# Weight splits ordered behind the steps of a recurrence, weights fetched earlier, and the samples' state products moved by a step: one layer of an RWKV-7 / short-convolution decoder

## The chip, the cores and the metric

The kernel runs on one core of a Trainium2 chip. The engines are TensorE (PE: matrix products; PEld its weight loads), VectorE (DVE: elementwise work), ScalarE (ACT: elementwise functions and copies), GpSimd (POOL) and SyncE (SP), whose queue issues most copies from DRAM. The metric is the device time of one execution in microseconds. PSUM is the memory that PE writes; it is shared out here in banks of 128 x 512 fp32.

## The reference: what is computed

One layer of a decoder, on 512 prompt tokens and on 8 samples of 4 tokens each (544 columns in all), fp32, model width 1024:

```python
x = layer_norm(ALPHA * x + 0.5 * swiglu(x, ffn1...))
proj = x @ w_in                          # 3328 columns: r, k, v, decay, a, gate | conv B, C, h
# RWKV-7: per head (8 heads of 64), per token
sa = S @ (-kk);  S = S * w + sa (kk*a)^T + v k^T;  o = S @ r
# group norm of o, bonus term, gate -> y_rwkv ; short convolution of width 3 -> y_conv
x = layer_norm(ALPHA * x + concat(y_rwkv, y_conv) @ w_out)
x = layer_norm(ALPHA * x + 0.5 * swiglu(x, ffn2...))
```

The outputs are the layer's result and the new states (the matrices S, the last shifted row, the last rows of the convolution), for the prompt and for the samples.

## The kernel before

Activations lie transposed: 128 rows of the model width on the partitions, tokens along the free axis, in two halves of 256 and 288 columns (`HALF`). Every large product is made of three matmuls: each fp32 operand is split in a high and a low part (both in PE's faster fp32r type), and high x high, high x low and low x high are summed. So each tile of weights (128 x 1024 fp32, 512 KB) is loaded into a raw buffer (`raw`, two of them in this part of the kernel), and then split by `wsplit`: ACT writes the high part (L135), DVE the low part, raw minus high (L136), into a tile `hl` (three of them, a fourth from the end of the first recurrence on). `wload` asks for the copy and the split; `wget` does so once for each tile of `w_in`. The low part's subtraction is what sets the raw buffer free for the next copy. `mm3` issues the matmuls of one output half: for 8 row blocks 24 matmuls, the low weights in every third of them (L154).

Between the two feed-forward blocks lies the mixer. The RWKV state recurrence is done by chunks of 64 tokens: for each of two groups of four heads (g = 0, 1) eight steps, `chain`, each of them a chain PE -> ACT -> PE -> DVE and ACT -> PE -> DVE:

- L1230: products of S (and of v) with the chunk's scores; ACT copies the result to W (L1233)
- L1239: W times the chunk's triangular inverse; DVE copies one half of the result into UV (L1240), ACT the other half (L1241)
- L1248: the state product; DVE adds it to S (L1256) and scales it (L1258). This last one is `upd` in the code
- L1209 and L1215: the chunk's outputs, of the step before; ACT copies them (L1217)

While the chain waits, PE gets other work, the fill: generators in a queue `bg`, from which `take(n)` draws about n ns of matmuls. `slots` alternates: it lets the chain write one step, then takes fill for that step (1500 in the recurrences). In recurrence 0 the fill is the projection for the convolution (`conv`, three tiles of `w_in` for each of four blocks: C, h, B, through `conv_mm`, each tile for both halves); in recurrence 1 it is the first part of the output product (`wout0`: for d = 0 to 7 four blocks of convolution rows from `wo_c[d // 2]`, and two blocks from `wo_0[d // 4]`), then `wout1` for the second half of the tokens. `last0` follows after recurrence 1 with the remaining two blocks. The pairs' own projections (`own_a`, `own_b`) are put in front of that queue where a pair of heads is due.

The samples (`sample`) are worked in between: `recur` calls `small(c, k)` at three places of each step c, which by a table `when` draws one or two pieces of the samples' work: two groups of 32 state products (L1293, one group for each pair of heads), copies, two small products, and then for each pair the new state (`ux` L1330, a product L1333, DVE L1335 and L1336). Two thirds into the recurrence the group norm of the first 256 tokens (`gnorm`, L1349 to L1369) is drawn too; that of the other 288 follows behind the recurrence.

The order of instructions on an engine is set by a scheduler when the program is built: among the instructions that it holds for ready by its own clock it takes the one that was written first. Two means hold it to an order on one engine: `after(a, b)` (a behind b) and `tc.issue_after(b)` (all that the block writes behind b). `slots` uses the second: the chain's matmuls are put behind the last fill matmul, and what a `take` writes is put behind the last product of the step on PE, and on ACT and DVE behind `seen["old"]`, the UV copy and the state product of the step before the one just written. The engines run the order as it was built, each instruction waiting for its operands.

Of the kernel before, what the change touches and what calls it, by code (L numbers as in the profile page):

```python
# [15 lines left out]
OP = mybir.AluOpType  # L16
# [45 lines left out]
def body(ctx: ExitStack, tc: tile.TileContext, xT, gu1, wd1, win, wo_c, wo_0, wo_1, gu2, wd2, wl, ln3, eye, lora, vec, cst,  # L62
# [71 lines left out]
    def wsplit(hl, raw, a, b):  # L134
        seen["hi"] = ACT.activation(hl[:, 0, a:b], raw[:, a:b], AF.Copy)  # L135
        seen["lo"] = DVE.tensor_tensor(hl[:, 1, a:b], raw[:, a:b], hl[:, 0, a:b].bitcast(F32), op=OP.subtract)  # L136
        return seen["lo"]

    def split(hi, lo, x):
# [16 lines left out]
                yield 6 * ((c1 - c0) / 2.4 + 3)  # L156

    bg = deque()
    seen = dict(rs=None, hhl=None, pe=None, fill=None, uv=None, new=[], old=[])

    def crit(e):
        seen["pe"] = e
# [1032 lines left out]
    def chain(g, cp, small):  # L1195


        tl = cp.tile
        AR = ARs[g]
        heads = [(pl, par) for pl in range(2) for par in range(2)]  # L1200
        Ss, q2, uv = {}, None, []

        def at(q, pl, par):
            return q[R(par), pl * 64:pl * 64 + 64]

        def out_u(c):
            q = sm()
            for pl, par in heads:
                crit(PE.matmul(at(q, pl, par), UV[:, pl, par, c, :], SC[:, pl, par, c, 64:128], start=(pl == 0 or c == 0),  # L1209
                               stop=(c == 0), skip_group_check=True))  # L1210
            return q

        def out_s(c, q):
            for pl, par in heads if c else ():
                crit(PE.matmul(at(q, pl, par), Ss[c][R(par), pl, par, :], AR[R(par), pl, c, 1, :], start=False, stop=True,  # L1215
                               skip_group_check=True))
            o = ACT.activation(O[:, :, c, :], v2(q), AF.Copy)  # L1217
            for e in uv:
                after(o, e)

        for c in range(8):
            if c < 7:
                Sn = Ss[c + 1] = tl([P, 2, 2, 64], F32, name="S", bufs=3)
                with tc.issue_after(seen["pool"].ins):
                    for par in range(2):
                        POOL.tensor_copy(Sn[R(1 - par), :, par, :], UV[R(1 - par), :, par, c + 1, :])
            q = sm()
            for pl, par in heads:
                k = slice(0, P) if c else R(1 - par)
                crit(PE.matmul(at(q, pl, par), SC[k, pl, par, c, 0:64], Ss[c][:, pl, par, :] if c else UV[k, pl, par, c, :],  # L1230
                               start=True, stop=True))
            W = tl([P, 2, 64], F32, name="W", bufs=2)
            ACT.activation(W, v2(q), AF.Copy)  # L1233
            if c:
                q2 = out_u(c - 1)
            small(c, 0)
            qs = (sm(), sm())
            for pl, par in heads:
                crit(PE.matmul(at(qs[par], pl, par), XT[R(par), c, pl, :], W[R(par), pl, :], start=True, stop=True))  # L1239
            seen["uv"] = DVE.tensor_copy(UV[R(0), :, 0, c, :], v2(qs[0], R(0)))  # L1240
            seen["new"] = [ACT.copy(UV[R(1), :, 1, c, :], v2(qs[1], R(1)))]  # L1241
            uv[:] = seen["new"]
            if c:
                out_s(c - 1, q2)
            small(c, 1)
            q = sm()
            for par, pl in heads:
                crit(PE.matmul(at(q, pl, par), BK[:, pl, par, c, :], UV[:, pl, par, c, :], start=True, stop=True))  # L1248
            pe = Pe[:, 2 * g:2 * g + 2, c:c + 1].to_broadcast([P, 2, 64])
            if c == 7:  # L1250
                SF = tl([P, 2, 64], F32, name="W", bufs=2)
            for par in range(2):
                dst = Sn[R(par), :, par, :] if c < 7 else SF[R(par)]
                src = v2(q, R(par))
                if c:
                    DVE.tensor_tensor(dst, Ss[c][R(par), :, par, :], src, op=OP.add)  # L1256
                    src = dst
                upd = DVE.tensor_tensor(dst, src, pe[R(par)], op=OP.mult)  # L1258
            seen["new"].append(upd)
            small(c, 2)  # L1260
            if c == 7:
                dma(wkvp_o[:, 2 * g:2 * g + 2, :], SF)
                out_s(7, out_u(7))
            yield 1

    def recur(g, cp, run):
        sam, gn = sample(g, cp), gnorm(g, 0, cp)
        when = {(2, 0): 1, (2, 1): 1, (2, 2): 1, (3, 0): 1, (3, 1): 1, (4, 2): 1, (5, 2): 2, (6, 2): 2}

        def small(c, k):  # L1270
            for _ in range(when.get((c, k), 0)):
# [9 lines left out]
    def sample(g, cp):  # L1281
# [3 lines left out]
        dma(S0, s0[:, 2 * g:2 * g + 2])  # L1285
        WT = tl([P, 2, 32], F32, name="WT")
        SI = tl([P, 2, 2, 64], F32, name="SI")
        q = sm()
        qv = q[:, :256].rearrange("p (d x t) -> p d x t", d=2, x=2)
        for pl in range(2):  # L1290
            for b in range(NSEQ):
# [48 lines left out]
    def gnorm(g, h, cp):  # L1340
# [13 lines left out]
            PE.matmul(q[:, :n], bo, sq[pl][:, :n], start=True, stop=True)  # L1354
            ACT.activation(sq[pl][:, :n], q[:, :n], AF.Ln, scale=1.0 / 64, bias=epsg)
        for pl in range(2):
            ACT.activation(sq[pl][:, :n], sq[pl][:, :n], AF.Exp, scale=-0.5)
        yield 600
        for pl in range(2):
            p = 2 * g + pl  # L1360
# [2 lines left out]
        for pl in range(2):  # L1363
            p, y = 2 * g + pl, sq[pl]
            DVE.scalar_tensor_tensor(y[:, :n], xc[pl][:, :n], col(V_GNG, p), sq[pl][:, :n], op0=OP.mult, op1=OP.mult)
            DVE.scalar_tensor_tensor(y[:, :n], y[:, :n], col(V_GNB, p), bvs[g][pl][:, t0:t1], op0=OP.add, op1=OP.add)
            DVE.tensor_tensor(o[pl], y[:, :n], qs[pl][:, :n], op=OP.mult)
            if g == 0:
                dma(ycd[:, p, t0:t1], o[pl])  # L1369
            else:  # L1370
# [19 lines left out]
    def conv(i):  # L1390
# [3 lines left out]
        us = u[:, 514:].rearrange("p (b t) -> p b t", t=6)  # L1394
        POOL.memset(u[:, 0:2], 0.0)
        POOL.tensor_copy(us[:, :, 0:2], cst_[:, i])
        for h in range(2):
            yield from conv_mm(14 + 3 * i, h, partial(conv_c, cc))
        for h in range(2):
            yield from conv_mm(15 + 3 * i, h, partial(conv_u, cc, u, us))  # L1400
        taps = conv_taps(i, u, us, zc)
        next(taps)
        for h in range(2):
            for n, x in enumerate(conv_mm(16 + 3 * i, h, partial(conv_z, zc))):
                if n in (0, 2):
                    next(taps, None)
                yield x
            for _ in taps:
                pass
        dma(ycd[:, 4 + i], zc)  # L1410

    def conv_mm(i, h, use):
        c0, c1 = HALF[h]
        w = wget(i)
        q = big()
        yield from mm3(q[:, :c1 - c0], w, xhl, range(KD), c0, c1)
        use(q, h, c0, c1)
        yield 300
# [80 lines left out]
    w4 = pool(ast, "w4")  # L1499
    wstate["ex_hl"] = [lambda: w4.tile([P, 2, 1024], F32R, name="hl", bufs=1)]  # L1500
    weave("s2", pairs[2].scores())
    bg.appendleft(own_b(3))
    need(3, 2)
    take(FILL["p3"])
# [42 lines left out]
            for k, y in ys + [(7, zc)]:  # L1547
                ysplit(k, y, c0, c1)

    w1s, fin = {}, []  # L1550

    def add_z(d, h, o, n=1):
        c0, c1 = HALF[h]
# [3 lines left out]
    def wout0():  # L1557
# [10 lines left out]
        for d in range(2):  # L1568
            yield from mm3(os[d][:, :c1], wc, xhl, (4, 5, 6, 7), c0, c1, d * 4, stop=False)
        for d in range(KD):  # L1570
            if d == 4:
                w0 = wload(wo_0[1])
            if d > 1:
                if d % 2 == 0:
                    wc = wload(wo_c[d // 2])
                o = big()
                yield from mm3(o[:, :c1], wc, xhl, (4, 5, 6, 7), c0, c1, (d % 2) * 4, stop=False)
            else:
# [20 lines left out]
    def wout1():  # L1599
# [8 lines left out]
        for d in range(KD):  # L1608
            if d == 4:
                w0 = wload(wo_0[1])  # L1610
            if d % 2 == 0:
                wc = wload(wo_c[d // 2])
            if d == 0:
                w0 = wload(wo_0[0])
            all_in = 3 in fin
            while all_in and rest:
                o = big()
# [48 lines left out]
    ast.close()  # L1666
    mst.close()
    yst.close()

    f2.s1[0] = s1  # L1670
    f2.open()
# [97 lines left out]
```

## Time and profile before

| | us |
|---|---|
| median of 3 runs | 1072.5 (1072.36 to 1072.72) |
| profiled execution: its time | 1072.43 |
| profiled execution: its span, first to last instruction | 1070.7 |
| recurrence 0: first L1230 to the last step's state product | 503.9 to 543.6 |
| recurrence 1 | 617.5 to 657.8 |
| a high part (ACT L135, mean of 230) | 1.02 |
| a low part (DVE L136, mean of 230) | 1.18 |
| granted clock of PE | 0.998 |

Rows of the timeline show start, duration, engine, line, operation, out <- in with shapes, a count where neighbours of one kind are merged, and in brackets how long the engine had idled and what released it. The durations of neighbours on one engine overlap by some tenths of a microsecond, because an instruction enters the pipe as the one before it leaves; what one costs in a row of work is the distance of the starts. PE's ends are modelled. A row of the waits names who waited, for whom, us in total, times, the longest.

### The profile page before, as it was taken

What the parts mean: (1) busy time and instruction counts of PE and PEld (TensorE: products, weight loads), DVE (VectorE), ACT (ScalarE), POOL (GpSimd) and SP (SyncE); (2) the same over time, 40 slices, a digit from 0 to 9 for tenths busy, and PEclk for the clock granted to TensorE, in tenths of its full rate; (3) what the DMA queues carried; (4) which work ended last, traced back from release to release, by engine and by line L of the source; (5) the groups of instructions that cost most, each with busy time, mean ns of one, the idle gap of its engine ahead of it and who ended that gap; (6) DMA issues with size and microseconds to landing.
All of it is one profiled execution on the core that took longest, in us unless ns stands there. A gap on an engine that the chain in (4) does not pass through costs nothing.

```text
span 1070.7 us, 22612 instructions
## 1 busy us (share of the span) xinstructions
PE 1050.7 (98%) x9178; PEld 1010.5 (94%) x9178; DVE 844.7 (79%) x1557; ACT 583.2 (54%) x1070; POOL 154.9 (14%) x273
## 2 busy tenths in 40 slices
PE   9999999999999999999999999999999999999997
PEld 8999999999999999899889988999999999999996
DVE  6797888979875777793578657988979888797757
ACT  5746555555553668654444435767555555555524
POOL 0111121211200022133101200001211212121000
PEclk9999999999999999999999999999999999999999
DMA  8558585676854233324145724434766848668512
GB/s 292 132 112 186 120 199 135 145 172 132 186 118 158 79 88 109 85 82 99 41 143 161 173 81 139 141 119 79 152 165 137 200 101 194 143 137 189 147 43 84
DMA packets 91528, 144.48 MB, mean 135 GB/s; under 512 B 34848, under 2 KB 52384, under 8 KB 91296
## 3 DMA queue, kind: packets, MB, share of 16 engines
q1 hardware_dynamic: 68144, 110.76, 34.2%
q0 software_dynamic: 22848, 31.72, 19.2%
q8 instruction: 72, 1.18, 0.4%
q10 hardware_dynamic: 432, 0.56, 0.2%
q14 instruction: 32, 0.26, 0.1%
HBM read 128.81 MB, written 9.75 MB: 129 GB/s over the span
## 4 chain that ended last, share of the span: by engine, by line
PE 76%; DVE 13%; ACT 7%; issue 2%; DMA 2%; POOL 0%; ACTq 0%; DVEq 0%; SPq 0%
PE mm L553 9%; PE mm L554 9%; PE mm L555 9%; PE sm L553 6%; PE sm L554 6%; PE sm L555 6%; PE mm L152 6%; PE mm L153 5%; PE mm L154 5%; DVE hhl L141 2%; ACT hl L135 2%; DVE hl L136 2%; PE sm L441 1%; PE sm L1166 1%; PE mm L784 1%
## 5 line engine op out<-in xcount | busy, mean ns | idle before, releaser
L136 DVE TENSOR_TENSOR hl<-raw,hl 128x1024 fp32r<-128x1024 f32 (+3 forms) x230 | 270.2, 1179 | 63.7 <-ACT hl L135 62.6
L135 ACT ACTIVATE hl<-raw 128x1024 fp32r<-128x1024 f32 (+3 forms) x230 | 232.9, 1020 | 69.7 <-DVE raw L519 43.5
L152 PE MATMUL mm<-xhl,hl 128*128 128x256 f32 (+1 forms) x704 | 209.2, 299 | 0.5 <-ACT xhl L140 0.5
L153 PE MATMUL mm<-xhl,hl 128*128 128x256 f32 (+1 forms) x704 | 203.0, 289 | 0.4 <-DVE xhl L141 0.4
L154 PE MATMUL mm<-xhl,hl 128*128 128x256 f32 (+1 forms) x704 | 202.0, 287 | 0.0
L152 PEld LDWEIGHTS mm<-xhl,hl 128*128 128x128 f32 x704 | 132.0, 188 | 6.9 <-issue 2.0
L153 PEld LDWEIGHTS mm<-xhl,hl 128*128 128x128 f32 x704 | 132.3, 188 | 2.7 <-issue 1.0
L154 PEld LDWEIGHTS mm<-xhl,hl 128*128 128x128 f32 x704 | 132.3, 188 | 0.3 <-issue 0.2
L555 PE MATMUL sm<-xhl,hl 128*128 128x272 f32 x432 | 125.2, 290 | 0.0
L554 PE MATMUL sm<-xhl,hl 128*128 128x272 f32 x432 | 124.4, 288 | 0.0
L553 PE MATMUL sm<-xhl,hl 128*128 128x272 f32 x432 | 124.1, 287 | 0.0
L553 PE MATMUL mm<-tv,hl 128*128 128x272 f32 x288 | 83.3, 289 | 0.3
L555 PE MATMUL mm<-tv,hl 128*128 128x272 f32 x288 | 83.4, 290 | 0.0
L554 PE MATMUL mm<-tv,hl 128*128 128x272 f32 x288 | 83.1, 288 | 0.0
L553 PEld LDWEIGHTS sm<-xhl,hl 128*128 128x128 f32 x432 | 81.4, 188 | 0.0
L554 PEld LDWEIGHTS sm<-xhl,hl 128*128 128x128 f32 x432 | 81.3, 188 | 0.0
L555 PEld LDWEIGHTS sm<-xhl,hl 128*128 128x128 f32 x432 | 81.2, 188 | 0.0
L532 POOL DMA_DIRECT2D raw<-in_wd x32 | 39.2, 1462 | 288.0 <-DVE hlb L141 225.2
L526 POOL DMA_DIRECT2D raw<-in_gu x36 | 43.3, 1203 | 203.5 <-DVE hlb L141 143.8
L553 PE MATMUL mm<-hhl,hl 128*128 128x272 f32 x192 | 56.4, 300 | 0.3
L554 PE MATMUL mm<-hhl,hl 128*128 128x272 f32 x192 | 55.9, 291 | 0.8 <-DVE hhl L141 0.2
L553 PEld LDWEIGHTS mm<-tv,hl 128*128 128x128 f32 x288 | 54.2, 188 | 1.9 <-ACT cpb L620 1.9
(416 smaller groups left out, 2716.0 us busy)
## 6 DMA issues: line engine op xcount, KB each, us to landing
raw<-in_gu SPq DMA_DIRECT2D x84, 512.0 KB, 4.5
raw<-in_gu POOLq DMA_DIRECT2D x36, 512.0 KB, 6.6
raw<-in_wd SPq DMA_DIRECT2D x32, 512.0 KB, 4.5
raw<-in_win SPq DMA_DIRECT2D x26, 512.0 KB, 3.6
raw<-in_wd POOLq DMA_DIRECT2D x32, 256.0 KB, 6.0
z<-sv POOLq DMA_DIRECT2D x16, 272.0 KB, 8.4
raw<-in_wo_c SPq DMA_DIRECT2D x8, 512.0 KB, 3.6
raw<-in_wd SPq DMA_DIRECT2D x8, 384.0 KB, 3.2
```

The source lines that it names most:

```text
L135: seen["hi"] = ACT.activation(hl[:, 0, a:b], raw[:, a:b], AF.Copy)
L136: seen["lo"] = DVE.tensor_tensor(hl[:, 1, a:b], raw[:, a:b], hl[:, 0, a:b].bitcast(F32), op=OP.subtract)
L141: return DVE.tensor_tensor(lo, x, hi.bitcast(F32), op=OP.subtract)
L152: PE.matmul(out, wh, src[:, 0, k, c0:c1], start=(start and i == 0), stop=False)
L153: PE.matmul(out, wh, src[:, 1, k, c0:c1], start=False, stop=False)
L154: seen["fill"] = PE.matmul(out, wl, src[:, 0, k, c0:c1], start=False, stop=(stop and i == n - 1))
L441: PE.matmul(o[i][h][:, :c1 - c0], block(hl, v, k), xhl[:, y, k, c0:c1], start=(k == 0 and j == 0), stop=(k == KD - 1 and j == 2), skip_gro ...
L526: POOL.dma_start(x.rearrange("p (s c) -> p s c", s=2), bass.AP(tensor=a11.tensor, offset=a11.offset, ap=[[2 * D, P], [P * 2 * D, 2], [1, 5 ...
L532: POOL.dma_start(four(x)[:, i], bass.AP(tensor=a11.tensor, offset=a11.offset, ap=[[DFF, P], [P * DFF, 2], [1, 256]]), accum_op=OP.add)
L553: PE.matmul(out, wh, src(0, i), start=(first and i == 0), stop=False, skip_group_check=True)
L554: PE.matmul(out, wh, src(1, i), start=False, stop=False, skip_group_check=True)
L555: PE.matmul(out, wl, src(0, i), start=False, stop=(i == n - 1), skip_group_check=True)
```

## The change

Five edits:

1. `wsplit`: while `seen["step"]` is set, the high part is ordered behind the UV copy on ACT, the low part behind the state product on DVE, of the step last written. `chain` sets it at the end of each step; `gnorm` sets it to its last product and its last exponential for the second part of the norm of group 0. It is cleared behind the scores of pair 2 and at the end of the mixer.
2. `conv_mm`: a tile's second half first asks for the next tile of the convolution (C to h, h to B, and B to the next block's C for the blocks 0 and 1).
3. `wout0`: `wo_c[1..3]` are asked for one d sooner, `wo_0[1]` two sooner, and the first two tiles of `wout1` at d = 6 and d = 7.
4. `recur`: the samples' first group of state products is drawn in step 1 behind the UV copy instead of in step 2, the second group and the copies one place sooner each, and the last state update in step 7 instead of step 6.
5. `sample`: the PSUM tile of the state products comes from `big` (three banks, the fill's) instead of `sm` (five banks, the chain's).

```diff
     def wsplit(hl, raw, a, b):
         seen["hi"] = ACT.activation(hl[:, 0, a:b], raw[:, a:b], AF.Copy)
         seen["lo"] = DVE.tensor_tensor(hl[:, 1, a:b], raw[:, a:b], hl[:, 0, a:b].bitcast(F32), op=OP.subtract)
+        if seen["step"]:
+            after(seen["hi"], seen["step"][1])
+            after(seen["lo"], seen["step"][0])
         return seen["lo"]
...
             seen["new"].append(upd)
+            seen["step"] = upd, uv[0]
             small(c, 2)
...
-        when = {(2, 0): 1, (2, 1): 1, (2, 2): 1, (3, 0): 1, (3, 1): 1, (4, 2): 1, (5, 2): 2, (6, 2): 2}
+        when = {(1, 1): 1, (2, 0): 1, (2, 1): 1, (3, 0): 1, (3, 1): 1, (4, 2): 1, (5, 2): 2, (7, 2): 2}
...
-        q = sm()
+        q = big()
         qv = q[:, :256].rearrange("p (d x t) -> p d x t", d=2, x=2)
...
-            ACT.activation(sq[pl][:, :n], sq[pl][:, :n], AF.Exp, scale=-0.5)
+            e = ACT.activation(sq[pl][:, :n], sq[pl][:, :n], AF.Exp, scale=-0.5)
...
-            DVE.tensor_tensor(o[pl], y[:, :n], qs[pl][:, :n], op=OP.mult)
+            m = DVE.tensor_tensor(o[pl], y[:, :n], qs[pl][:, :n], op=OP.mult)
+            if h and not g:
+                seen["step"] = m, e
...
+        j = 14 + 3 * i
         for h in range(2):
-            yield from conv_mm(14 + 3 * i, h, partial(conv_c, cc))
+            yield from conv_mm(j, h, partial(conv_c, cc), j + 1)
         for h in range(2):
-            yield from conv_mm(15 + 3 * i, h, partial(conv_u, cc, u, us))
+            yield from conv_mm(j + 1, h, partial(conv_u, cc, u, us), j + 2)
...
-            for n, x in enumerate(conv_mm(16 + 3 * i, h, partial(conv_z, zc))):
+            for n, x in enumerate(conv_mm(j + 2, h, partial(conv_z, zc), j + 3 if i < 2 else 0)):
...
-    def conv_mm(i, h, use):
+    def conv_mm(i, h, use, nxt=0):
         c0, c1 = HALF[h]
         w = wget(i)
+        if h and nxt:
+            wget(nxt)
         q = big()
...
     weave("s2", pairs[2].scores())
+    seen["step"] = None
...
         for d in range(KD):
+            if d % 2 == 0 and d:
+                wc = wn
             if d == 4:
-                w0 = wload(wo_0[1])
+                w0 = w0n
+            if d == 2:
+                w0n = wload(wo_0[1])
+            if d in (1, 3, 5):
+                wn = wload(wo_c[d // 2 + 1])
+            if d == 6:
+                pre.append(wload(wo_c[0]))
+            if d == 7:
+                pre.append(wload(wo_0[0]))
             if d > 1:
-                if d % 2 == 0:
-                    wc = wload(wo_c[d // 2])
                 o = big()
...
             if d == 4:
                 w0 = wload(wo_0[1])
-            if d % 2 == 0:
+            if d == 0:
+                wc, w0 = pre
+            elif d % 2 == 0:
                 wc = wload(wo_c[d // 2])
-            if d == 0:
-                w0 = wload(wo_0[0])
...
     yst.close()
+    seen["step"] = None
```

More of the change, by code (lines that the diff above doesn't have):

```diff
@@ L158, in body @@
     bg = deque()
-    seen = dict(rs=None, hhl=None, pe=None, fill=None, uv=None, new=[], old=[])
+    seen = dict(step=None, rs=None, hhl=None, pe=None, fill=None, uv=None, new=[], old=[])
     def crit(e):
@@ L1548, in conv_last @@
                 ysplit(k, y, c0, c1)
-    w1s, fin = {}, []
+    w1s, fin, pre = {}, [], []
     def add_z(d, h, o, n=1):
```

## The prediction, made before the run

> **What bounds the kernel now.** I read the page first, then the waits of TensorE (PE) from 500 to 680 us, then one row per recurrence step from the windows view, then the timeline around each hole.
>
> ```profile
> span 1070.7 us, 22612 instructions
> ...
> PE 1050.7 (98%) x9178; PEld 1010.5 (94%) x9178; DVE 844.7 (79%) x1557; ACT 583.2 (54%) x1070; POOL 154.9 (14%) x273
> ```
>
> PE is idle for 20.0 us of 1070.7. The change removes no arithmetic, so a gain can only come out of idle time, and only near the two recurrences and the stage behind the first. The two largest waits that it can reach:
>
> ```profile
> PE sm L1248 <- DVE UV L1240: 3.4, 8, 0.7
> ...
> PE sm L1057 <- DVE gq L1365: 0.6, 1, 0.6
> ```
>
> L1248 is the state product of a step; it waits until VectorE (DVE) has copied UV. By step (columns: stretch, length, then busy time of PE, PEld, DVE, ACT, POOL):
>
> ```profile
> 508.30:513.00 4.70, 4.16 (x52) 3.60 (x50) 2.60 (x6) 1.76 (x4) 0.00 (x0) 1.00 0.00 0
> ...
> 523.40:528.30 4.90, 4.68 (x69) 4.18 (x68) 3.62 (x10) 0.97 (x4) 0.63 (x3) 1.00 0.40 107
> ...
> 540.90:544.20 3.30, 2.58 (x58) 2.22 (x57) 2.70 (x6) 0.82 (x3) 0.00 (x0) 1.00 0.56 149
> 552.40:561.00 8.60, 7.96 (x101) 6.50 (x100) 6.80 (x13) 2.94 (x10) 0.00 (x0) 1.00 0.46 129
> 617.40:621.90 4.50, 3.75 (x46) 3.20 (x46) 1.70 (x5) 0.54 (x2) 0.00 (x0) 1.00 0.39 120
> 621.90:626.20 4.30, 3.79 (x53) 3.31 (x52) 2.37 (x7) 2.71 (x5) 0.00 (x0) 1.00 0.00 0
> ...
> 636.30:641.20 4.90, 4.49 (x67) 4.01 (x66) 3.66 (x10) 0.82 (x3) 0.57 (x2) 1.00 0.39 106
> ...
> 648.70:654.50 5.80, 5.21 (x61) 4.34 (x60) 5.67 (x13) 1.87 (x4) 0.00 (x0) 1.00 0.55 162
> ```
>
> These are, in order: steps 1, 4 and 7 of recurrence 0 (PE idle 0.54, 0.22, 0.72), the scores behind it (0.64), and steps 0, 1, 4 and 6 of recurrence 1 (0.75, 0.51, 0.41, 0.59). The ceiling of the whole edit is thus about 4 us, 0.4% of the time.
>
> **The change part by part.** *T1, the samples' state products one place sooner.* 32 products go from step 2 between the second product and L1248 into step 2's first place, and 32 from there into step 1.
>
> ```profile
> 510.04 0.46 PE L1248 MATMUL sm<-UV,BK 128*64 128x64 f32 x8 [0.37 <-DVE UV L1240]
> ...
> 513.63 1.10 PE L1293 MATMUL sm<-AR,DM 64*64 64x8 f32 x32
> ...
> 536.24 0.45 PE L1239 MATMUL sm<-W,XT 64*64 64x64 f32 x8
> 537.05 0.46 PE L1248 MATMUL sm<-UV,BK 128*64 128x64 f32 x8
> ```
>
> In step 1 nothing of PE lies between L1239 and L1248; 1.10 us of products cover that hole of 0.37. Step 2 loses its second group, and is left like step 6, where only L1215 lies there and about 0.13 stays open (L1239's other matmuls and L1215 end at 536.92; L1248 starts at 537.05). Net 0.37 - 0.13 = 0.24 per recurrence, the hole of recurrence 1 being alike (its step 1 idles 0.51 in all): -0.47 together. Bounds: -0.73 (nothing opens in step 2) to 0. The products read S0, whose load moves too:
>
> ```profile
> 616.49 0.33 SPq L1285 DMA_DIRECT2D DM<-in_s  x1
> ```
>
> ```profile
> DMA to landing us min/median/max: 3.7/4.4/5.1
> ```
>
> It already waits at SP's head until DM is free, so it is issued no sooner: 616.49 + 5.1 = 621.6 at worst, before step 1 opens at 621.90. The PSUM tile that moves from `sm` to `big` leaves two of three `mm` banks to the fill; a half needs one while the previous one is being drained, so I cost it at 0 (one DVE copy, 0.3, per recurrence if that cover goes). The last two state updates move from step 6 to step 7, off a full DVE queue.
>
> *T2, step 7 of recurrence 0.* DVE between the state product of step 6 and the UV copy of step 7:
>
> ```profile
> 538.27 0.60 DVE L1258 TENSOR_TENSOR S<-S,Pe 64x128 f32<-64x128 f32 x2
> ...
> 539.51 1.22 DVE L136 TENSOR_TENSOR hl<-raw,hl 128x1024 fp32r<-128x1024 f32 x1
> ...
> 541.64 1.22 DVE L136 TENSOR_TENSOR hl<-raw,hl 128x1024 fp32r<-128x1024 f32 x1
> 542.78 0.27 DVE L1240 COPY UV<-sm 64x128 f32<-64x128 f32 x1
> ```
>
> Two weight splits and two updates of S0 fill that stretch; the second split ends after UV could be copied. It belongs to the last pair's projection, 20 us before its use at 562. In the new order conv 2's second tile is asked for before it and is held behind the group norm's last product, and its raw copy waits for the first split. So one split and both updates leave: 2.4 us of DVE. The hole goes from 0.72 to the 0.13 of step 6: -0.58; bounds -0.72 and 0.
>
> *T3, the norm behind recurrence 0.*
>
> ```profile
> 551.69 1.06 ACT L135 ACTIVATE hl<-raw 128x1024 fp32r<-128x1024 f32 x1 [0.70 <-DMA raw<-in_win]
> 552.65 0.43 ACT L1357 ACTIVATE gq<-gq 128x288 f32<-128x288 f32 x1
> ```
>
> ```profile
> 552.78 1.23 DVE L136 TENSOR_TENSOR hl<-raw,hl 128x1024 fp32r<-128x1024 f32 x1 [0.52 <-ACT hl L135]
> ...
> 553.92 0.51 DVE L1365 SCALAR_TENSOR_TENSOR gq<-sm,vc,gq 128x288 f32<-128x288 f32 x1
> ```
>
> A split stands before the norm's exponential on ACT and before L1365 on DVE; L1365 frees the PSUM bank that the scores wait for. The new code orders splits traced here behind both. The same 36 score products (L1057 alone; stretch, length, PE busy) take 3.02 + 0.64 here and 2.28 where no norm precedes:
>
> ```profile
> 552.40:556.20 3.80, 3.02 (x36) 2.45 (x36) 1.00 0.38 95
> 570.00:572.50 2.50, 2.28 (x36) 2.11 (x36) 1.00 0.11 31
> ```
>
> So 1.38 is there to win, 0.64 of it plain idle. The split then competes with the evictions of the scores (L1060), so I take 0.64 and half of the other 0.74: -1.0; bounds -1.38 and 0. The tile held back is used at 568, 12 us later.
>
> *T4, what is lost: the second w_out tile in step 0 of recurrence 1.* `wout0` fetches `wo_c[1]` at d = 1, in the fill that follows step 0, and uses it at d = 2 of the same fill. Today the split is free to run at once, here long before:
>
> ```profile
> 600.83 1.23 DVE L136 TENSOR_TENSOR hl<-raw,hl 128x1024 fp32r<-128x1024 f32 x1 [0.62 <-ACT hl L135]
> ...
> 619.64 0.61 DVE L1258 TENSOR_TENSOR S<-sm,Pe 64x128 f32<-64x128 f32 x2 [0.57 <-PE sm L1248]
> 620.53 0.42 DVE L1555 TENSOR_TENSOR z<-z,mm 128x256 f32<-128x256 f32 x1 [0.28 <-PE mm L154]
> ```
>
> ```profile
> 618.82 0.26 ACT L1241 COPY UV<-sm 64x128 f32<-64x128 f32 x1 [0.57 <-PE sm L1239]
> ```
>
> ```profile
> 620.33 0.28 PE L152 MATMUL mm<-xhl,hl 128*128 128x256 f32 x1
> ...
> 620.56 0.28 PE L154 MATMUL mm<-xhl,hl 128*128 128x256 f32 x1
> ```
>
> Now the high part goes behind the UV copy (619.08 + 1.06 = 620.14, in time for the matmul at 620.33), the low part behind the state product: 620.27 + 1.23 = 621.50. The low matmul due at 620.56 waits until about 621.55: +1.0. Everything behind it on PE waits too (step 1's L1230 is ordered behind this fill), so nothing covers it. If the z addition at 620.53 goes first, +1.6; if the scheduler found other fill, 0. I take +1.0, since the split is traced first.
>
> *T5, splits whose place hardly moves.* A split was already held behind the products of the step before the last one; now it is held behind the last one, but traced one take sooner. For conv 1's third tile, conv 2's first and `wo_c[3]` the two cancel. Steps 4 and 6 therefore keep their holes:
>
> ```profile
> 636.85 1.22 DVE L136 TENSOR_TENSOR hl<-raw,hl 128x1024 fp32r<-128x1024 f32 x1
> 637.98 0.28 DVE L1240 COPY UV<-sm 64x128 f32<-64x128 f32 x1
> ```
>
> The split is already behind the state product of step 3; what it delays is the UV copy of step 4, and no line of the diff puts it behind that. I take 0; bounds: -1.22 (0.22 + 0.41 + 0.59) to 0. The Trainium skill, page "TensorE: Matmul & The Clock Gate", section "Architectural detail", states that ScalarE and VectorE take their queue strictly in order; by that rule a place behind step c protects nothing of step c + 1 and these holes stay, while an engine that could pass the copy ahead would bring the sum 1.22 lower. The trace sides with the rule: the copy starts where the split's overlapped tail ends.
>
> *Sum*: -0.47 - 0.58 - 1.0 + 1.0 + 0 = -1.05. The profiled execution took 1072.43 in all (span 1070.7), 0.07 under the median of 1072.5, so 1072.5 - 1.05 = **1071.5 us**.
>
> **Rivals.** *A, the UV copies come free everywhere.* The splits that move ahead of the sample's products of ux and S0 leave DVE idle when UV is due in steps 4 and 6, and T3 comes in full: a further -1.22 - 0.38, 1069.9. For it: the split now has an earlier place than ux. Against it: DVE's work between the state product and the copy stays the same in sum in those steps.
>
> *B, recurrence 1 starves for weights.* There are two raw buffers. `wo_c[1]` and `wo_0[1]` now sit in them until step 0's products, so `wo_c[2]` can be asked for at 621.5; today it is asked for at about 605.
>
> ```profile
> raw<-in_gu POOLq DMA_DIRECT2D x36, 512.0 KB, 6.6
> ...
> raw<-in_wo_c SPq DMA_DIRECT2D x8, 512.0 KB, 3.6
> ```
>
> It lands at 625.1 to 628.1, and is split 2.3 later if the engines are free, 627.4 to 630.4; its first low matmul is due at about 631. If it misses the UV copy of step 2 it falls behind that step's products (4 times 0.3) and is some 1.8 late. With T4 at 1.6 that is +1.6 + 1.8 instead of +1.0: 1073.9, and up to 1075.7 if `wo_c[3]` inherits the lateness. It decides when the copy lands later than about 627.5. Against it: the median landing leaves 3 us.
>
> *C, the change doesn't do what it says.* If the lag of T5 cancels in T2 and T3 too, and `wo_c[1]` is covered, only T1 is left: 1072.0.
>
> **How the numbers follow.** Forecast 0.52 (own range 1070.5 to 1072.9), A 0.20, B 0.20, C 0.08. A run of this kernel can tell about 0.2%, 2.1 us, from no change: below 1070.4 counts as faster, above 1074.6 as slower. Faster: most of A and a tail of the forecast, 0.20. Slower: a good half of B and some room for a stall elsewhere, 0.16. Same: 0.64. The range runs from A's time to the upper half of B: 1069.7 to 1074.6.
>
> **What would show it.** T1: step 1 of both recurrences holds 32 products of L1293 and no hole before L1248; a hole of about 0.1 in step 2. T2: one split between the products of step 6 and the UV copy of step 7, S0's last update after it. T3: no split before the last L1365; the wait of L1057 on it is gone. T4: a wait of PE on DVE L136 of about 1 us near 620.5, which today's list doesn't have. T5: the waits of L1248 in steps 4 and 6 unchanged. Wrong would be: no such wait in step 0, several waits on L136, or a time outside the range, above all by a stage outside 500 to 660 us.

## The result, and the profile after

The changed kernel took 1079.98 us in the median of five runs (1078.04 to 1080.54) beside 1072.72 for the kernel before: a ratio of 1.0061, 95% interval 1.005 to 1.0072. In a second set of six runs it took 1079.77 beside 1073.05 (1.0052, 1.0035 to 1.007). It is slower by some 7 us where 1 us less was forecast, and outside the forecast's range of 1069.7 to 1074.6.

The page of the changed kernel's profiled execution (1078.04 us in all):

```profile
span 1076.3 us, 22603 instructions
...
PE 1054.5 (98%) x9178; PEld 1013.2 (94%) x9178; DVE 845.4 (79%) x1557; ACT 583.3 (54%) x1070; POOL 159.6 (15%) x273
```

The number of matmuls is the same, yet PE is busy for 3.8 us more: the same matmuls took longer. Its waits from 500 to 680 us (who waits, for whom, us in total, times, longest; line numbers are 3 or 4 higher than before, so that L1251 is the old L1248, L1063 the old L1060, L1074 the old L1071):

```profile
PE sm L1251 <- DVE UV L1243: 2.0, 5, 0.6
PE sm L1074 <- DVE SC L1063: 1.3, 2, 1.0
PE sm L1093 <- DVE SC L1063: 1.2, 1, 1.2
PE mm L157 <- DVE hl L136: 0.8, 1, 0.8
...
PE sm L1060 <- DVE bkb L1040: 0.7, 1, 0.7
```

The state product's waits fell from 3.4 us to 2.0, as planned. The other four rows are new or longer: two on the evictions of scores (L1063; of the first, 0.3 us stood there before, as L1071), one on a low weight part (L136) in recurrence 1, and one on `bkb`. An eviction here is DVE's multiplication that takes a bank of scores out of PSUM, and so sets the bank free. The waits on L1063 and `bkb` lie between the recurrences. The windows view of stretches shown before (stretch, length, then busy time of PE, PEld, DVE, ACT, POOL, then the granted clock, the share of the DMA engines and GB/s):

```profile
508.30:513.00 4.70, 4.70 (x83) 4.38 (x82) 1.43 (x5) 0.86 (x4) 0.00 (x0) 1.00 0.33 112
540.90:544.20 3.30, 3.16 (x44) 2.07 (x39) 2.34 (x7) 0.82 (x3) 0.31 (x1) 1.00 0.62 171
...
552.40:561.00 8.60, 7.39 (x83) 5.98 (x79) 6.43 (x12) 1.53 (x3) 0.00 (x0) 0.84 0.68 187
```

Step 1 of recurrence 0 has no hole any more (0.54 before), step 7 has 0.14 (0.72 before). The scores behind it idle for 1.21 us instead of 0.64, and there the granted clock is no longer 1.00. Where the two profiled executions part, by the start of the same instruction in each:

| | before | after | difference | change since the line above |
|---|---|---|---|---|
| first product of recurrence 0 | 503.93 | 504.20 | +0.27 | |
| first score product of pair 2 (the third pair) | 552.47 | 552.06 | -0.41 | -0.68 |
| projection fill behind pair 2's scores | 562.01 | 565.15 | +3.14 | +3.55 |
| products of `nk` behind pair 3's scores (L1103, now L1106) | 579.01 | 583.93 | +4.92 | +1.78 |
| first product of recurrence 1 | 617.48 | 622.39 | +4.91 | -0.01 |
| first sum behind `last0` (L231, now L234) | 673.78 | 679.54 | +5.76 | +0.85 |

So recurrence 0 gained most of what was forecast, and 5.3 us were lost in 32 us between the recurrences. DVE and PE there, from the timeline (start, duration, engine, line, out <- in, count, idle before and what ended it):

```profile
552.63 0.45 DVE L1371 TENSOR_TENSOR O<-gq,sm 128x288 f32<-128x288 f32 x1
553.00 1.22 DVE L136 TENSOR_TENSOR hl<-raw,hl 128x1024 fp32r<-128x1024 f32 x1
554.13 1.28 DVE L1063 TENSOR_TENSOR SC<-sm,cs 128x512 f32<-128x512 f32 x2
555.33 1.22 DVE L136 TENSOR_TENSOR hl<-raw,hl 128x1024 fp32r<-128x1024 f32 x1
556.46 1.48 DVE L1063 TENSOR_TENSOR SC<-sm,cs 128x512 f32<-128x512 f32 x3
```

```profile
555.25 0.74 PE L1074 MATMUL sm<-cs,bkb 64*128 64x64 f32 x10
557.20 0.32 PE L1093 MATMUL sm<-cs,v 64*64 64x64 f32 x2 [1.21 <-DVE SC L1063]
```

The norm's last operation (L1371) now runs ahead of both splits, as the change intends, and the score products run in one go. But the two splits stand one ahead of the six evictions of the scores and one in the middle of them. The ten transposes of L1074 fill the two banks that the first two evictions set free; at 555.99 PE has no free bank of `sm`, and the next transposes (of v, L1093) wait for the third eviction. What follows is PE alone, in stretches cut where the granted clock changes (length, PE busy, granted clock, DMA):

```profile
554.92:558.33 3.41, 2.20 (x24) 1.00 0.78 191
558.33:561.75 3.42, 3.42 (x34) 0.50 0.71 200
561.75:565.16 3.41, 3.41 (x17) 0.50 0.00 0
```

For 6.83 us PE runs at half its clock. At most half of that, 3.4 us, is lost to it; in the profiled execution of the kernel before, the clock is 1.00 throughout this stretch. Pair 3's scores then wait three times, 2.03 us in all, where before PE idled for 0.78 us from 570 to 579:

```profile
575.08 2.13 PE L1060 MATMUL sm<-AR,bkb 64*128 64x128 f32 x33 [0.72 <-DVE bkb L1040]
...
578.35 0.27 PE L1074 MATMUL sm<-cs,bkb 64*128 64x64 f32 x1 [0.98 <-DVE SC L1063]
578.95 0.52 PE L1074 MATMUL sm<-cs,bkb 64*128 64x64 f32 x9 [0.33 <-DVE SC L1063]
```

```profile
576.47 1.22 DVE L136 TENSOR_TENSOR hl<-raw,hl 128x1024 fp32r<-128x1024 f32 x1
```

Here too a split runs while PE needs a bank: it stands ahead of all six evictions, the first of which starts at 577.60. One stood there before (571.16). What is new is that `bkb` comes late, and that PE has no fill. On DVE one split more (571.11) and the two masks of L1125 (565.12, 568.83) now stand between L1107, the last work on pair 2, and the part of `bkb` that PE waits for (L1040). It starts 9.40 us behind the first L1107, instead of 7.26 us behind that operation before.

This is the first of three fill matmuls that stood between scores and transposes of pair 3 in the kernel before; none of them is there now:

```profile
572.31 0.39 PE L152 MATMUL mm<-xhl,hl 128*128 128x256 f32 x1
```

Of the five runs none had a mean clock above 0.996 (the two at 0.996 took 1078.0 to 1078.2 us, the three at 0.992 took 1080.0 to 1080.5). The kernel before may not be free of it: of its 74 executions beside the experiments 24 had 0.997 or less, though none of these was traced. But there such an execution takes 1.4 us more (medians of 1072.6 and 1074.0), and of the changed kernel's eleven executions ten are at 0.996 or less.

### The profile page after: what moved, and what is told of

Read it like the earlier page. It is cut to its first block, busy times and chain, and to the rows that moved or that the text cites. A ratio compares the mean times of both kernels' runs of the same rounds, so it can differ in the third digit from the quotient of the medians.

```text
span 1076.3 us, 22603 instructions
## 1 busy us (share of the span) xinstructions
PE 1054.5 (98%) x9178; PEld 1013.2 (94%) x9178; DVE 845.4 (79%) x1557; ACT 583.3 (54%) x1070; POOL 159.6 (15%) x273
## 4 chain that ended last, share of the span: by engine, by line
PE 77%; DVE 14%; ACT 6%; issue 2%; DMA 1%; POOL 0%; ACTq 0%; DVEq 0%; SPq 0%
PE mm L556 9%; PE mm L557 9%; PE mm L558 9%; PE mm L155 6%; PE sm L556 6%; PE sm L557 6%; PE sm L558 6%; PE mm L156 6%; PE mm L157 6%; DVE hhl L144 2%; DVE hl L136 2%; PE sm L444 1%; ACT hl L135 1%; PE sm L1169 1%; PE mm L787 1%
## 5 line engine op out<-in xcount | busy, mean ns | idle before, releaser
L136 DVE TENSOR_TENSOR hl<-raw,hl 128x1024 fp32r<-128x1024 f32 (+3 forms) x230 | 270.5, 1179 | 59.6 <-ACT hl L135 58.5
```

## The experiments

The first theory: the hold behind the norm and the early request of the convolution tiles together put two splits into pair 2's evictions; PE is idle for 1.21 us, the clock falls, and this is most of the loss. Rivals: that the waits on VectorE alone cost and the clock is chance; that recurrence 1 starves for `w_out`. Each ratio is to the kernel before on the same chip.

**1. No hold behind the norm.**

```diff
             m = DVE.tensor_tensor(o[pl], y[:, :n], qs[pl][:, :n], op=OP.mult)
-            if h and not g:
-                seen["step"] = m, e
```

> The changed kernel without the hold of the split behind the norm of recurrence 0 (the split goes where it stood before), all else as changed. Theory (two splits in front of the evictions of pair 2's scores leave TensorE idle for 1.21 us, and the granted clock is then 0.50 for 6.9 us): the wait at the transposes' consumers of pair 2 falls under 0.4 us, the granted clock is 1.00 from 550 to 600 us, and of the 5 us lost between 552 and 587 us some 4 come back, less the 1.4 us of the wait ahead of the norm that opens again: 1075 to 1077 us. Rival 'only the VectorE wait, the clock is chance': the wait goes and the wait ahead of the norm comes back, 1079 to 1080 us, the clock at 0.50 somewhere all the same. Rival 'recurrence 1 starves for w_out': no change, 1079 to 1080 us.

Measured: 1075.35 us (ratio 1.0021, 1.001 to 1.0032). Five of twelve executions had a clock of 0.998 or more, called whole from here on, median 1073.5; seven had less, median 1077.2. The wait in pair 2's scores did not go away:

```profile
552.98 1.29 DVE L1063 TENSOR_TENSOR SC<-sm,cs 128x512 f32<-128x512 f32 x2 [0.17 <-PE sm L1060]
554.91 1.23 DVE L136 TENSOR_TENSOR hl<-raw,hl 128x1024 fp32r<-128x1024 f32 x1 [0.64 <-ACT hl L135]
556.05 1.48 DVE L1063 TENSOR_TENSOR SC<-sm,cs 128x512 f32<-128x512 f32 x3
```

```profile
553.81 1.06 ACT L135 ACTIVATE hl<-raw 128x1024 fp32r<-128x1024 f32 x1 [2.91 <-DMA raw<-in_win]
```

```profile
556.79 0.33 PE L1093 MATMUL sm<-cs,v 64*64 64x64 f32 x2 [1.29 <-DVE SC L1063]
```

One part of the theory falls: it needs no two splits and no hold. The time was as forecast, the reason was not. With the early request and no hold behind the norm a raw copy lands at 553.8, and its one split goes between the second and the third eviction: 1.29 us idle. In this profiled execution the clock stayed whole all the same, so an idle gap of that size does not bring it down each time. Nor did the wait ahead of the norm come back; no split stands there.

**2. No early request** of the next convolution tile, the hold kept.

```diff
         w = wget(i)
-        if h and nxt:
-            wget(nxt)
```

> The changed kernel without the early request of the next convolution tile; the hold behind the norm and the rest stay. Theory: behind the norm one split stands instead of two, so that the wait in pair 2's scores is about half of 1.21 us (0.3 to 0.7), too short to bring the clock down: granted clock 1.00 from 550 to 600 us, 1074 to 1076 us. Rival 'the hold alone does it': the wait stays near 1.2 us and the clock still falls to 0.50, 1078 to 1081 us. Rival 'recurrence 1 starves': no change, 1079 to 1080 us.

Measured: 1076.82 us (1.0033, 1.0021 to 1.0045), so all three statements missed in one way or another: pair 2's scores wait for nothing at all, and the loss is somewhere else, in recurrence 0:

```profile
517.28 0.38 PE L155 MATMUL mm<-xhl,hl 128*128 128x256 f32 x1 [1.01 <-ACT hl L135]
...
518.87 0.52 PE L157 MATMUL mm<-xhl,hl 128*128 128x256 f32 x1 [1.09 <-DVE hl L136]
```

```profile
515.55:518.96 3.41, 1.17 (x16) 1.00 0.00 0
518.96:522.38 3.42, 3.42 (x16) 0.50 0.48 153
```

Held behind the steps and asked for at the old time, a tile comes too late for its fill. The early request is what makes the new places possible, and it is also what brings a split to the scores. The clock falls here too, 38 us ahead of pair 2's first score product and without any norm nearby: behind a stretch in which PE idled for 2.24 us of 3.41. So the fall is not bound to the place.

**3. Work in the wait.** The wait on VectorE stays, PE gets something to do in it.

```diff
+                if p == 2 and not a0c:
+                    dq = big()
+                    with tc.issue_after(tr.ins):
+                        for _ in range(8):
+                            PE.matmul(dq[:, :288], xhl[:, 0, 0, 0:P], xhl[:, 0, 0, 256:544], start=True, stop=True)
                 if a0c:
```

> The changed kernel with eight more products of 128x288 whose result nobody reads, in the order of TensorE behind the ten transposes of pair 2, where it is idle for 1.21 us (8 x 0.13 = 1.04 us). Theory: the wait on VectorE is as long as before, but TensorE has work in it, the granted clock stays 1.00 and, although work is added, the time falls by about 3.4 us: 1075.5 to 1077.5 us. Rival 'only the waits on VectorE cost, the clock falls for another reason': the time stays or rises by up to 1 us, 1079.5 to 1081 us, and the clock is still 0.50 for 6.9 us near 558 us.

Measured: 1075.65 us (1.0025, 1.0016 to 1.0033). Eight of eleven executions had a clock of 0.998 or more. The eight products are L1080, the next transposes (of v) L1098 and L1099 here:

```profile
555.62 1.32 PE L1080 MATMUL mm<-xhl 128*128 128x288 f32 x8
556.90 0.33 PE L1098 MATMUL sm<-cs,v 64*64 64x64 f32 x2
557.49 0.24 PE L1099 MATMUL sm<-cs,v 64*64 64x64 f32 x1 [0.27 <-DVE SC L1063]
```

```profile
554.92:558.33 3.41, 3.14 (x33) 1.00 0.80 209
558.33:565.16 6.83, 6.49 (x64) 1.00 0.49 132
```

A kernel with more work took 4.3 us less (1075.65 against 1079.98, the difference to the kernel before falling from 7.3 to 2.9). That cannot be a wait on VectorE: its split is at the same place (555.02) and of the same length (1.22). It is the clock. The rival of the waits alone falls.

**4. `w_out`'s second tile asked for ahead of recurrence 1.**

```diff
         w0 = wload(wo_0[0])
+        wn = wload(wo_c[1])
...
-            if d in (1, 3, 5):
+            if d in (3, 5):
                 wn = wload(wo_c[d // 2 + 1])
```

> The changed kernel with the second tile of w_out of recurrence 1 asked for ahead of the recurrence, not in its step 1. Theory: the 0.83 us stall at the first low product of step 1's fill goes and nothing else: 1079.0 to 1079.5 us, the clock at 0.50 near 558 us as in the changed kernel. Rival 'recurrence 1 starves for w_out and this is the larger loss': 1077 us or less.

Measured: 1079.02 us (1.0049, 1.0037 to 1.0061), 0.8 to 1.0 us under the changed kernel's two medians, which the intervals don't tell apart. The waits do: the stall of 0.83 us is not among them, and no other on a weight part takes its place. The rival falls. Its profiled execution shows two falls of the clock:

```profile
555.55:558.96 3.41, 2.42 (x23) 1.00 0.81 245
558.96:562.38 3.42, 3.42 (x33) 0.50 0.40 103
...
576.03:579.44 3.41, 2.68 (x25) 1.00 0.96 272
579.44:582.85 3.41, 3.41 (x33) 0.50 0.71 194
```

The second lasts until 586.27 and follows pair 3's three waits, so pair 3's scores too can be followed by a fall.

The theory now read: a split between the second and the third eviction of pair 2's scores leaves PE idle for about 1.2 us; the clock then often falls, behind pair 2 and behind pair 3. Open were whether it can be made to happen in the kernel before, whether the place of that one split explains the loss, and what the moved products are worth alone.

**5. The moved products alone.** The kernel before with the new table `when` and `q = big()` in `sample`, and nothing else of the change.

```diff
-        when = {(2, 0): 1, (2, 1): 1, (2, 2): 1, (3, 0): 1, (3, 1): 1, (4, 2): 1, (5, 2): 2, (6, 2): 2}
+        when = {(1, 1): 1, (2, 0): 1, (2, 1): 1, (3, 0): 1, (3, 1): 1, (4, 2): 1, (5, 2): 2, (7, 2): 2}
...
-        q = sm()
+        q = big()
         qv = q[:, :256].rearrange("p (d x t) -> p d x t", d=2, x=2)
```

> The kernel before with the samples' products alone moved: the new table of their places and the PSUM tile from the other pool, none of the new waits of the splits, no early requests. In its order of VectorE one split stands ahead of pair 2's score evictions and none among them, and TensorE has 63 products of the projections ahead of pair 3's scores, as before (72 in the changed kernel). Theory (the loss is a split among the evictions, and the clock behind it): step 1's hole closes in both recurrences (-0.47), the norm's exponentials and L1365 run ahead of the split (-0.6 to -1.0), no stall in the scores of more than 0.4 us, clock 0.998 or 0.999: 1071.0 to 1072.0 us, the fastest so far. Rival 'the moved products cost something that the other edits hid': 1073 us or more.

Measured: 1070.54 us (0.9976, 0.9967 to 0.9985), faster than both kernels and 0.5 us below the range expected; nine of ten executions had a clock of 0.998 or more. Its DVE at the end of the norm and the waits of its PE from 500 to 680 us:

```profile
550.14 0.52 DVE L1365 SCALAR_TENSOR_TENSOR gq<-sm,vc,gq 128x288 f32<-128x288 f32 x1 [2.46 <-ACT gq L1357]
...
551.13 0.52 DVE L1365 SCALAR_TENSOR_TENSOR gq<-sm,vc,gq 128x288 f32<-128x288 f32 x1
...
552.36 1.22 DVE L136 TENSOR_TENSOR hl<-raw,hl 128x1024 fp32r<-128x1024 f32 x1
...
553.86 2.48 DVE L1060 TENSOR_TENSOR SC<-sm,cs 128x512 f32<-128x512 f32 x4
```

```profile
PE sm L1248 <- DVE UV L1240: 2.4, 6, 0.6
...
PE sm L1091 <- DVE SC L1060: 0.5, 2, 0.3
```

The wait on the norm (0.64 before) is gone without any hold: the order as built has both L1365 ahead of the split, and the split as a whole ahead of the evictions, none among them. That this comes of the last state updates leaving step 6 is likely and was not tested. No wait in the scores is longer than 0.33 us. So this one edit closes step 1's hole in both recurrences (T1), brings 0.2 of T2 (step 7's hole is 0.50) and 1.16 of the 1.38 us that T3 was after (from pair 2's first score product to its first transpose, 3.42 us instead of 4.58). Recurrence 1 and what follows, up to the first sum behind `last0`, is 1.0 us shorter, where T1 asked for 0.24; what the rest is was not looked into. The rival falls.

**6. Longer evictions in the kernel before.**

```diff
                                       (msk if n > 1 else msks)[:, None, :].to_broadcast([P, n, P]), op=OP.mult)
+                if p == 2 and not a0c:
+                    for par in range(2):
+                        x = SC[:, pl, par, 0:4, :]
+                        DVE.tensor_tensor(x, x, msk[:, None, :].to_broadcast([P, 4, P]), op=OP.mult)
```

> The kernel before with two more VectorE operations between the second and the third eviction of pair 2's scores: they multiply the mask in once more (2 x 0.68, overlapped 1.28 us), which changes no value; in its order TensorE has 65 products ahead of pair 3's scores. Theory (an idle TensorE of some 1.2 us among small products there can bring the clock down): a wait of 1.0 to 1.3 us on the third eviction; in runs in which the clock stays whole 1073.5 to 1074 us, in others 1076 to 1078 us with a granted clock of 0.993 to 0.996 over the run, at least one such run in five. Rival 'the clock falls for something else in the changed kernel (the splits, the transfers, the held norm)': the same wait, 1073.5 to 1074 us in all runs, clock 0.998 throughout.

Measured: 1075.65 us (1.0024, 1.0015 to 1.0033); six executions at 0.998 or more, median 1074.9 (1 us above what was expected), five at 0.996 or 0.997, median 1075.9. The wait is 0.83 us, a little less than expected, and in the profiled execution the clock fell behind it:

```profile
558.16 0.33 PE L1094 MATMUL sm<-cs,v 64*64 64x64 f32 x2 [0.83 <-DVE SC L1060]
```

```profile
557.37:560.78 3.41, 2.62 (x27) 1.00 0.37 81
560.78:564.19 3.41, 3.41 (x30) 0.50 0.02 4
```

So a fall behind pair 2's scores can be had in the kernel before, with no split among the evictions, no early request and no held norm. It is weaker evidence than hoped for, since the kernel before, on the same chip, had 10 of 28 executions at 0.997 or less.

**7. The split held behind the evictions**, with the edit of experiment 4; **8. the same alone**. At the norm the low parts written from there on are noted, and the two copies that follow the evictions hold them:

```diff
         if seen["step"]:
             after(seen["hi"], seen["step"][1])
             after(seen["lo"], seen["step"][0])
+        if seen["held"] is not None:
+            seen["held"].append(seen["lo"])
...
-                seen["step"] = m, e
+                seen["step"], seen["held"] = (m, e), []
...
-                        DVE.tensor_copy(dst, src)
+                        cb = DVE.tensor_copy(dst, src)
+                        if par:
+                            for lo in seen["held"]:
+                                after(lo, cb)
+                            seen["held"], seen["step"] = None, (cb, seen["step"][1])
```

> The changed kernel with the split that stands among pair 2's evictions held behind the two VectorE copies that follow them (VectorE idles there for 1.2 us before the change), and the second tile of w_out asked for ahead of recurrence 1. One split still stands ahead of the first eviction, and TensorE has 72 products ahead of pair 3's scores as in the changed kernel. Theory: pair 2's wait falls from 1.21 to 0.3 us or less, the clock stays whole there, the 0.83 us stall on w_out is gone; what is left of the loss is pair 3's (its order is unchanged), 0.5 to 1.5 us: 1072.0 to 1074.0 us. Rival 'pair 3 and its missing 9 products are the larger part': 1075.5 us or more, with waits of 2 us there and the clock down behind them.

> The changed kernel with one edit alone: the split that stands among pair 2's evictions is held behind the two copies that follow them; w_out stays as changed. Theory: the time of the kernel with both edits (1071.4 to 1072.2 us where the clock stayed whole, 1074.4 to 1076.8 us elsewhere) plus the 0.83 us stall on w_out: 1072.3 to 1073.1 us with a whole clock, median 1074.5 to 1076 us, that is 4 to 5 us under the changed kernel. Rival 'w_out's tile was the larger part of what that kernel won': 1078 us or more.

Measured: 1074.65 us with both edits (1.0009, 0.9998 to 1.002), 0.65 above what was expected, and 1075.56 with the hold alone (1.0013, 1.0003 to 1.0024), as expected. DVE of the second:

```profile
552.74 1.23 DVE L136 TENSOR_TENSOR hl<-raw,hl 128x1024 fp32r<-128x1024 f32 x1
553.88 2.67 DVE L1065 TENSOR_TENSOR SC<-sm,cs 128x512 f32<-128x512 f32 x5
...
556.67 0.88 DVE L1083 COPY BK<-sm 128x320 f32<-128x320 f32 x2
557.46 1.22 DVE L136 TENSOR_TENSOR hl<-raw,hl 128x1024 fp32r<-128x1024 f32 x1
```

The same split, at the same length, 2.1 us later: pair 2's wait falls from 1.21 to 0.27 us, and the time by 4.2 (1075.56 against 1079.77 on the same chip). Five of twelve executions, in both kernels, had a clock of 0.998 or 0.999: median 1072.2 and 1072.8. Their difference of 0.7 is an upper price of `w_out`'s tile, since the kernel before differed by 0.2 between the two chips (1072.5 and 1072.7 in such executions). The other seven had 0.993 to 0.996 and medians of 1075.5 and 1076.4. Pair 3's wait of 0.94 us is still there in the profiled executions, whose clock is whole. That it is this wait behind which the clock falls in the seven fits experiment 4, but no trace of such an execution was taken.

**9. Experiment 6 with eight products in the wait** (the lines of experiments 3 and 6 together).

> The kernel before with the two extra mask multiplications between pair 2's evictions and, in TensorE's wait for them, eight products of 128x288 whose result nobody reads (8 x 0.13). Theory (idle TensorE brings the clock down): the runs at 1075.6 to 1076.7 us with a clock of 0.996 that the kernel with the longer evictions showed in about half of its executions get rare; median 1074.3 to 1075.2 us, clock 0.998 or 0.999 in nearly all. Rival 'VectorE's delay costs and the clock follows from something else': half of the runs stay at 0.996 and the median at 1075.6 us or, with 1 us of added products, above.

Measured: 1074.03 us (1.0013, 1.0005 to 1.0022), four of eleven executions at 0.996 or less. The median is 1.6 us lower than without the products, as the theory asks, and 0.3 us below the range expected, but the executions with a lower clock are hardly rarer (four of eleven against five). This one does not tell the two apart: the order as built changed as well, and a wait of 0.94 us on the norm (L1374) stands ahead of the scores.

**10. The changed kernel once more.**

> The changed kernel once more, for the spread of its clock beside the two kernels of this call. Theory: 1078 to 1080.5 us in nearly all executions, the clock between 0.992 and 0.996, one or two falls of it near 558 and 580 us, at moments that lie whole multiples of 3.41 us apart. Rival 'the fall of the clock was chance in the first five runs': a third of the executions or more at 0.998 or above, 1075 us or less.

Measured: 1079.77 us; one of six executions had a clock of 0.999, and took 1075.39, the others 0.992 to 0.996 and 1077.65 to 1081.83. Its profiled execution:

```profile
557.11:563.94 6.83, 6.83 (x50) 0.50 0.45 116
...
581.00:587.83 6.83, 6.83 (x42) 0.50 0.72 170
```

The fall is no chance of the first five runs. The one execution without it gives the two parts of the loss: about 2.6 us over the kernel before are waits (1075.39 against 1072.74, the kernel before's median where the clock is whole), the other 4 to 5 us are the clock. It is one execution, but experiment 3's eight with a whole clock lie at the same time (median 1075.3).

## Why the prediction was wrong

**T1** (samples' products one place sooner, -0.47) was right: no hole in step 1, 0.14 opens in step 2, in both recurrences.

**T2** (step 7, -0.58) was right: 0.72 became 0.14. With T1's half it is 0.82 of gain in recurrence 0; the landmarks show 0.68.

**T4** (`wo_c[1]` late, +1.0) was right in its mechanism and place, and measured 0.83 of idle time, 1.0 in the distance of the starts (due at 625.47):

```profile
626.47 0.39 PE L157 MATMUL mm<-xhl,hl 128*128 128x256 f32 x1 [0.83 <-DVE hl L136]
```

Experiment 4 prices it at 0.8 to 1.0, 7 against 8 at 0.7 at most. Only this one tile was late, so rival B did not come.

**T5** (steps 4 and 6 keep their holes) was right: the five waits of L1251 that are left are 0.37 in the first step of each recurrence, 0.23 in step 4 of recurrence 0, and 0.41 and 0.58 in steps 4 and 6 of recurrence 1. Rival A did not come. Rival C did not either: the change does what it says.

**T3 is the step that failed**: "The split then competes with the evictions of the scores (L1060), so I take 0.64 and half of the other 0.74: -1.0; bounds -1.38 and 0." The competitor was named and then priced as a smaller gain, never as a loss. The gain did come, in full: the score products ran in 2.28 us, and the first transpose behind them started 1.8 us sooner, of which 0.41 came from recurrence 0 and 1.39 from the norm. What the bounds left out:

- Where the split stands among the evictions. Ahead of all of them it cost pair 2's scores next to nothing (experiments 2, 5 and 8: waits of 0.3 us or less). Between the second and the third it stands exactly where PE runs out of banks, and costs 1.21 to 1.29 us, its whole length. Nor is a place ahead of all of them free by itself: pair 3's scores, with no fill between, waited 0.98 us behind such a split.
- That the early request, in the prediction only a help to T2, brings a split to that place even without the hold behind the norm (experiment 1).
- That what is late goes on: PE waits 0.7 to 1.0 us for pair 3's `bkb`, and the order as built has 72 fill matmuls ahead of pair 3's scores instead of 63, which leaves none for the waits inside them: +1.78 us, of which 1.25 is idle time of PE. No experiment changed pair 3's order, so this part is read from the trace.
- The clock. Every term was a sum of waits at full speed. Of some 7 us lost 4 to 5 are matmuls at half the clock (experiments 3 and 10). The prediction said that it would be wrong "above all by a stage outside 500 to 660 us"; the loss was inside, and of a kind that no row of the profile before could have shown, since its clock was 0.998 and its largest idle gap there 0.64 us.

Most of the chance for slower was given to rival B, a starving recurrence 1. The true mechanism, a split as a wait in the scores, was a clause in the working of a gain and no rival.

Open: why the scheduler placed the splits and pair 3's fill as it did in each kernel was read from the built order, not tested. What exactly decides whether the clock falls was not tested either; the last section has what the traces say of it.

## What to carry to other kernels

When a piece of work on an in-order engine is held back, look for the next instruction behind which another engine runs out of buffers, and price the held piece at its full length there, as a loss; then move it to a place where that engine idles. A wait of PE of about a microsecond among small products can cost more than its length, since the matmuls of the next 3 to 7 us may run at half the clock: judge such a change by the granted clock of many executions, and try filling the wait with products, as experiment 3 did. And try the edits of a bundle one by one: here the moved products with their PSUM tile gave 2 us, and the other edits more than took it back.

## What the hardware showed that was not expected

The granted clock of PE falls to 0.50, for 3.41 or 6.83 us, and comes back with PE busy all along. In the seven falls traced here (experiments 2, 4 twice, 6, 10 twice, and the first profile) PE had been idle for 0.73 to 2.24 us of the 3.41 before. Two falls in one execution lie 20.48 us apart (558.96 and 579.44) or 23.89 (557.11 and 581.00), that is 6 and 7 times 3.41: they fit a grid that runs on by itself. The Trainium skill, page "TensorE: Matmul & The Clock Gate", section "Part 1: The HAM clock gate", describes such a free-running window, 3413 ns long, and these traces agree with its length. It puts the loss of the full clock behind at least one idle window of about 3.4 us; here 0.73 us of idle time in a stretch of small products was followed by one, so the measurement decides.

The grid holds in all twelve traces: within each, all changes of the clock lie whole multiples of 3.4133 us apart, to 0.01 us. The same gap does not always bring a fall: experiment 1's of 1.29 us had none. A limit of the grid at 556.11 cuts it, so that the two stretches have 0.61 and 0.75 us of idle time.

Idle time on the grid does not decide by itself, though. Stretches with 1.24 us (the changed kernel, from 623.18), 1.25 us (experiment 3, from 569.27) and 1.27 us (experiment 8, from 570.28) were followed by no fall, and one with 0.73 us was. What sorts them far better is how much PE has to do in a stretch, counted as the columns that its matmuls write (64 for a row 64x64, 288 for a row 128x288). Of the 3634 stretches at full clock from 20 to 1060 us in the twelve traces, with 7344 columns in the median, the six with the fewest (1280 to 2816) are all followed by a fall, and the seventh fall follows one with 3072, among the eleven lowest. The two stretches of experiment 1's gap have 4928 and 3712, more than any of the seven. By this count a wait harms most among small products, and experiment 3's eight products add 2304 columns. This was read from the traces afterwards, in which a few matmuls can be missing; no run tested it.
